# Rounded parts for the late half of u, and loads by pairs of chunks, in a decoder trunk

## The chip, the cores and the metric

The kernel runs on one core of one Trainium2 chip. The metric is the device time of one execution in microseconds (us); the time before is the median of 3 runs, 1722.25 us (1722.04 to 1727.37). The timeline and all rows come from one further execution that a hardware profiler recorded.

## What is computed

A block of a hybrid decoder for 512 tokens of width 1024: a recurrent branch (HGRN2) and a sparse-attention branch, merged by gates, then an expert layer (PEER). All values are float32. What matters here is the expert layer:

```python
def peer_ffn(x, w_q, sub_keys, u, v):          # u, v: 16384 experts x 1024
    q = (xb @ w_q).reshape(TB, H, 2, PEER_HALF)
    s = jnp.einsum('thpc,phnc->thpn', q, sub_keys)
    ...                                        # per token 8 heads x 16 experts: eidx, and softmax weights g
    ug = u[eidx]
    vg = v[eidx]
    h = jnp.einsum('tkd,td->tk', ug, xb)
    a = jax.nn.gelu(h, approximate=False) * g
    return jnp.einsum('tk,tkd->td', a, vg)
```

The result is added to the residual stream, which a last RMS norm scales.

## The kernel before, in words

The kernel is written in tile pools: each named tile has a ring of buffers, and a planner orders the instructions of each engine at build time, so an engine's order is near that of the program but not the same. On the chip every engine works through its list in order.

Up to about 460 us the kernel does the two branches and the residual. Then comes the expert layer, in two forms at once. For the first 192 tokens it **gathers**: `row` (L773) fetches, for each of the 192 slots (128 of the first block, 64 of a half block folded on 128 partitions), one row of u (`u_row`, L780: one VectorE instruction with a sum) and later one row of v (`v_row`, L792: one VectorE multiply-add into `acc`). That is 384 gathers of 512 KB, issued by GpSimd into the ring `row` of 6 buffers (L766). For the other 320 tokens (T0 on) it computes **densely** over all experts, in 128 chunks of 128 experts:

- `query` (L652) and `picks` (L689), with the first 22 chunks of u between them (from 464 to 703 us).
- The rest of the early half of u up to chunk 63 (loop at L890), with `g_group` (L860), which spreads the expert weights into a dense table `g_d` in DRAM through `stg`.
- `chunk(q)` (L987) for q = 0 to 127: loads v ahead (`v_load`), multiplies chunk q + 66 of u while there is one (`u_chunk`, L756), makes the parts of v (`v_parts`, L920), and multiplies (`v_product`, L942, and once for two chunks `v_halves`, L948). For q from 0 to 61 u and v stand together; from 62 on there is v alone, with the GELU of the early half of u read back from `h_d`.

`u_chunk` is 8 plain float32 matmuls of 320 columns; the profile has two records for each of them. `v_product` uses **rounded parts**: `hi` is v rounded to fp32r by a ScalarE copy (L925), `lo` the rest by a VectorE subtraction (L926), the same for the activations (`aH` L937, `aL` L939), and `mm3` (L74) makes three fp32r matmuls of 512 columns, L77 to L79, of them. `v_halves` is plain float32 on 64 columns of weights, 8 records for a pair of chunks.

Loads of u and wq go through the ring `u_raw` (4 buffers of 512 KB, L637), those of v through `v_raw` (8 buffers, L831), one DMA of 512 KB for each chunk, all in SyncE's queue. ScalarE's queue carries the writes and reads of `h_d`, the reads of `g_d` and small loads. The gathers are spread by `some_rows` (L803): R0, R1, R2 and R3 are the gathers for each chunk in the four stretches (2, 2, 3.2 and 0.9), with none for the last NOROW = 4 chunks of the early half; what is left is done at q = 120 (`last_rows`, L978). `issue_after` puts their instructions on VectorE behind the last `pace[0]` of the program so far.

Of the kernel before, what the change touches and what calls it, by code (L numbers as in the profile page):

```python
# [10 lines left out]
F32 = mybir.dt.float32  # L11
F32R = mybir.dt.float32r
# [6 lines left out]
OP = mybir.AluOpType  # L19
# [21 lines left out]
def trunk(ctx, tc, A, out, dbg=None):  # L41
    nc = tc.nc
    dve, act, pool, pe, sync = nc.vector, nc.scalar, nc.gpsimd, nc.tensor, nc.sync
# [70 lines left out]
    pace = [None, None]  # L114
# [11 lines left out]
    ps = psum([P, S], "hg")  # L126
# [505 lines left out]

    LEAD, UH, AHEAD = 64, [2, 2, 3, 3, 3, 3, 3, 3], 2
    UPRE = sum(UH)
    R0, R1, R2, R3, NOROW = 2, 2, 3.2, 0.9, 4
    TG, QJ, VR = 32, 4, 8
    ust = ctx.enter_context(tc.tile_pool(name="ust", reuse_waits="tile", bufs=4))  # L637

    def raw_weight(src):
        raw = ust.tile([P, 1024], F32, name="u_raw")  # L640
        sync.dma_start(raw, src)
        return raw.rearrange("p (c m) -> p c m", c=8)
# [8 lines left out]

    def query(m, w=S):  # L652

        raw = raw_weight(A["peer_wq"][m])
# [111 lines left out]
    gp = ctx.enter_context(tc.tile_pool(name="gp", reuse_waits="tile", bufs=6))  # L766
    wk = ctx.enter_context(tc.tile_pool(name="wk4", reuse_waits="tile", bufs=2))
    hh = wk.tile([P, P + HT], F32, name="hh", bufs=1)
    ah = wk.tile([P, P + HT], F32, name="ah", bufs=1)
    scr = wk.tile([P, D], F32, name="scr", bufs=1)  # L770
# [54 lines left out]
    weigh()  # L825
    rks.close()
    pps.close()


    up = ctx.enter_context(tc.tile_pool(name="up", reuse_waits="tile", bufs=2, space=PSUM))  # L830
    vt = ctx.enter_context(tc.tile_pool(name="vt", reuse_waits="tile", bufs=VR))  # L831
    with ExitStack() as st:
        gt = st.enter_context(tc.tile_pool(name="gt", reuse_waits="tile", bufs=1))
        gq = st.enter_context(tc.tile_pool(name="gq", reuse_waits="tile", bufs=2))
# [55 lines left out]
        for j in range(UPRE, LEAD):  # L890
# [13 lines left out]
    act.dma_start(gfin, bass.AP(tensor=A["norm_final"].tensor, offset=A["norm_final"].offset, ap=[[0, P], [1, D]]))  # L904
# [7 lines left out]
    raws = {}  # L912
    order = list(range(LEAD, P)) + list(range(LEAD))

    def v_load(q):
        if q < P:
            raws[q] = vt.tile([P, D], F32, name="v_raw")
            sync.dma_start(raws[q], v3[:, order[q], :])

    def v_parts(q, hgt):  # L920
        j = order[q]
        raw = raws.pop(q)
        vh = vx.tile([P, D], F32R, name="v_hi")
        vl = vx.tile([P, D], F32R, name="v_lo")
        act.copy(vh, raw)  # L925
        dve.tensor_tensor(vl, raw, vh.bitcast(F32), op=OP.subtract)  # L926
# [12 lines left out]
        pace[0] = dve.tensor_tensor(aL, gj[:, HT:], aH.bitcast(F32), op=OP.subtract)  # L939
        return gj, raw, (aH, aL), (vh, vl)  # L940
# [13 lines left out]

    def total(b, src, n):

        if n == 0:
            fin[b] = [vt.tile([P, D], F32, name="v_raw").rearrange("p (n d) -> p n d", n=2), vs.tile([P, 2], F32, name="ss")]
# [4 lines left out]
        dve.tensor_tensor(g[:, n, :], xs, gfin[:, n * 512:(n + 1) * 512], op=OP.mult)  # L963

    def finish(b):

# [10 lines left out]

    def last_rows():  # L978
        some_rows(len(rows) + len(vrows) + 1)
        for n in range(2):  # L980
            total(0, acc[0][:, n * 512:(n + 1) * 512], n)
        finish(0)

    for q in range(VR - 3):
# [28 lines left out]
    hs = vt.tile([P, D], F32, name="v_raw").rearrange("p (n d) -> p n d", n=2)  # L1013
    for n in range(2):
        act.copy(hs[:, n, :], hacc[n])
    for b in range(2):
# [100 lines left out]
```

## Time and profile before

| | before |
|---|---|
| median of the runs | 1722.25 us (1722.04 to 1727.37) |
| profiled execution: its time | 1719.29 us |
| profiled execution: span of the core | 1717.5 us |
| TensorE (PE) busy in the span | 1665.5 us, 97% |
| VectorE (DVE) busy | 1290.4 us, 75% |
| ScalarE (ACT) busy | 562.5 us, 33% |
| GpSimd (POOL) busy | 531.5 us, 31% |
| moved by DMA | 465.11 MB, mean 271 GB/s |

How to read it: the span lies within the time, with 1.8 us around it. PE is matmul, PEld the weight loads beside it. The page cuts the span into 40 slices and gives the busy share of each in tenths, PEclk the granted clock of TensorE (10 tenths is 2.4 GHz), DMA the mean share in which the 16 DMA engines had a packet. That share is counted from packet times, which overlap a little, so it can pass 1. A matmul's record is longer than its turn, since matmuls are pipelined: its pace is read from start to start.

### The profile page before, as it was taken

The numbers are of one execution on the slowest core, as the hardware profiler recorded it, in microseconds if no ns is written. First come the engines' busy times: TensorE is split into PE (matmuls) and PEld (weight loads), VectorE is DVE, ScalarE is ACT, GpSimd is POOL, SyncE is SP. The second block draws the span as 40 slices with busy tenths as digits, with TensorE's granted clock in tenths as the row PEclk, the third lists the DMA queues.
The fourth block names the chain that finished last, engine by engine and source line by source line (L and its number), as shares of the span: only waits on it lengthen the run. The fifth ranks groups of instructions, "written<-read, shape, count | busy, mean of one in ns | idle before, by whom it ended". The sixth has DMA issues, their size and how long they took to land.

```text
span 1717.5 us, 21753 instructions
## 1 busy us (share of the span) xinstructions
PE 1665.5 (97%) x7551; PEld 1181.0 (69%) x7553; DVE 1290.4 (75%) x2601; ACT 562.5 (33%) x895; POOL 531.5 (31%) x413
## 2 busy tenths in 40 slices
PE   8999999999899999899999999999999999999997
PEld 6988887778765556576776666666666666666663
DVE  4776878447369999988785787777777777888787
ACT  4422237644321111444443222222222222333333
POOL 2000000000021313255552456554454454333231
PEclk9999999999999999999999999999999999999999
DMA  6422143136665666699999999999999999999993
GB/s 231 139 74 61 62 154 105 50 108 198 200 220 201 233 212 204 216 412 417 401 393 337 346 401 381 368 347 365 362 348 365 360 346 328 361 357 341 357 351 118
DMA packets 179437, 465.11 MB, mean 271 GB/s; under 512 B 16728, under 2 KB 76504, under 8 KB 177920
## 3 DMA queue, kind: packets, MB, share of 16 engines
q1 hardware_dynamic: 52560, 200.32, 32.1%
q0 software_dynamic: 55296, 201.35, 31.2%
q10 hardware_dynamic: 71472, 62.07, 11.5%
q8 instruction: 59, 0.97, 0.2%
q14 instruction: 50, 0.41, 0.1%
HBM read 425.31 MB, written 40.39 MB: 271 GB/s over the span
## 4 chain that ended last, share of the span: by engine, by line
PE 71%; DVE 11%; DMA 9%; issue 4%; POOL 3%; ACT 1%; ACTq 0%; SPq 0%; POOLq 0%; DVEq 0%
PE ps_u L759 17%; PE acc L77 7%; PE hacc L951 7%; DMA row<-in_peer_u,eidx 7%; PE acc L78 6%; PE acc L79 6%; PE ps_mm L77 5%; PE ps_mm L79 5%; PE ps_mm L78 5%; PE ps_mm L661 2%; POOL row L776 2%; PE ps_hg L759 2%; PE ps_hg L380 2%; DVE scr L782 1%; PE ps_hg L77 1%
## 5 line engine op out<-in xcount | busy, mean ns | idle before, releaser
L759 PE MATMUL ps_u<-xfT,u_raw 128*128 128x320 f32 x1696 | 483.8, 439 | 4.3 <-ACT hg L761 4.3
L759 PEld LDWEIGHTS ps_u<-xfT,u_raw 128*128 128x128 f32 x1696 | 319.6, 192 | 150.9 <-ACT v_hi L925 20.3
L776 POOL DMA_INDIRECT row<-in_peer_u,eidx x128 | 175.7, 1372 | 319.8 <-DVE hh L782 257.9
L798 DVE SCALAR_TENSOR_TENSOR acc<-row,ah,acc 128x1024 f32<-128x1024 f32 x190 | 244.5, 1287 | 2.0
L776 POOL DMA_INDIRECT row<-in_peer_v,eidx x128 | 165.8, 1295 | 239.7 <-DVE acc L798 225.2
L77 PE MATMUL acc<-v_hi,aH 128*128 128x512 f32 x512 | 219.7, 429 | 1.2 <-ACT aH L937 1.2
L78 PE MATMUL acc<-v_lo,aH 128*128 128x512 f32 x512 | 200.7, 392 | 0.4 <-DVE v_lo L926 0.4
L79 PE MATMUL acc<-v_hi,aL 128*128 128x512 f32 x512 | 199.8, 391 | 0.0
L782 DVE CUSTOM_DVE_ANT_0 scr<-row,xf 128x1024 f32<-128x1024 f32 x128 | 156.4, 1222 | 37.2 <-DMA row<-in_peer_u,eidx 35.3
L926 DVE TENSOR_TENSOR v_lo<-v_raw,v_hi 128x1024 fp32r<-128x1024 f32 x128 | 156.0, 1220 | 36.2 <-ACT v_hi L925 35.3
L925 ACT CAST v_hi<-v_raw 128x1024 fp32r<-128x1024 f32 x128 | 134.0, 1047 | 148.8 <-PE acc L79 96.7
L761 ACT ACTIVATE hg<-ps_u 128x320 f32<-128x320 f32 x106 | 46.4, 438 | 345.0 <-PE ps_u L759 343.3
L77 PEld LDWEIGHTS acc<-v_hi,aH 128*128 128x128 f32 x512 | 96.2, 188 | 52.5 <-ACT v_hi L925 24.3
L951 PE MATMUL hacc<-v_raw,aj 128*64 128x512 f32 x512 | 126.6, 605 | 0.9 <-DVE aj L934 0.9
L109 ACT CAST w_hi<-w_raw 128x1024 fp32r<-128x1024 f32 (+3 forms) x71 | 68.3, 962 | 152.9 <-PE ps_mm L78 66.6
L71 POOL TENSOR_TENSOR rs_r<-rs_ms,half 128x1 f32<-128x1 f32 (+1 forms) x13 | 10.8, 829 | 339.7 <-DVE rs_ms L69 328.7
L78 PEld LDWEIGHTS acc<-v_lo,aH 128*128 128x128 f32 x512 | 96.4, 188 | 22.8 <-DVE v_lo L926 0.7
L661 PE MATMUL ps_mm<-xfT,u_raw 128*128 128x512 f32 (+1 forms) x288 | 111.9, 547 | 0.0
L79 PEld LDWEIGHTS acc<-v_hi,aL 128*128 128x128 f32 x512 | 96.2, 188 | 22.0 <-DVE aL L939 0.6
L776 POOL DMA_INDIRECT row<-in_peer_v,eidh x64 | 82.3, 1286 | 78.8 <-DVE acc L798 58.5
L776 POOL DMA_INDIRECT row<-in_peer_u,eidh x64 | 88.0, 1375 | 57.3 <-DVE hh L782 46.1
L77 PE MATMUL ps_mm<-xnH,w_hi 128*128 128x512 f32 (+1 forms) x248 | 100.8, 406 | 0.0
(306 smaller groups left out, 2611.3 us busy)
## 6 DMA issues: line engine op xcount, KB each, us to landing
u_raw<-in_uT SPq DMA_DIRECT2D x128, 512.0 KB
v_raw<-in_peer_v SPq DMA_DIRECT2D x128, 512.0 KB
g_d<-stg SPq DMA_DIRECT2D x10, 2048.0 KB
gj<-g_d ACTq DMA_DIRECT2D x32, 640.0 KB
w_raw<-in_wT SPq DMA_DIRECT2D x31, 512.0 KB
h_d<-hg ACTq DMA_DIRECT2D x64, 160.0 KB
hgr<-h_d ACTq DMA_DIRECT2D x64, 160.0 KB
w_raw<-in_w_out SPq DMA_DIRECT2D x16, 512.0 KB
```

The source lines that it names most:

```text
L77: pe.matmul(ps, lh, rh, start=first, stop=False, **kw)
L78: pe.matmul(ps, lh, rl, start=False, stop=False, **kw)
L79: pe.matmul(ps, ll, rh, start=False, stop=last, **kw)
L109: act.copy(hi[:, :n], raw[:, :n])
L661: pe.matmul(ps[:, ts], raw[:, c, :], xfT[:, c, ts], start=(c == 0), stop=(c == 7))
L759: pe.matmul(ps[:, :NT], raw[:, c, :], xfT[:, c, T0:], start=(c == 0), stop=(c == 7))
L776: pool.indirect_dma_start(out=g, out_offset=None, in_=A[tab], in_offset=bass.IndirectOffsetOnAxis(ap=ap, axis=0))
L782: dve.tensor_tensor_reduce(out=scr, in0=row("peer_u", half, k), in1=xfh if half else xf0, scale=1.0, scalar=0.0, op0=OP.mult, op1=OP.add, ...
L798: dve.scalar_tensor_tensor(acc[half], row("peer_v", half, k), s, acc[half], op0=OP.mult, op1=OP.add)
L925: act.copy(vh, raw)
L926: dve.tensor_tensor(vl, raw, vh.bitcast(F32), op=OP.subtract)
L951: pe.matmul(hacc[n][z * HT:(z + 1) * HT, :], gj[:, :HT], raw[:, n * 512:(n + 1) * 512], start=first, stop=last)
```

## The change

Five things change. (1) For chunks of u from 64 on, `u_chunk` makes `hi` and `lo` of the raw chunk by the new `parts` (one ScalarE copy and one VectorE subtraction of 128 x 1024, as for v) and multiplies them by `mm3` with parts of the tokens, `xfp`, which are made once behind `weigh()` (128 x 2560 on each engine): 24 fp32r matmuls of 320 columns in place of 8 plain ones. (2) u and v share one ring of parts, `w_hi` and `w_lo`, of 3 buffers each; before, `v_hi` and `v_lo` had 2 each. (3) wq, u and v are loaded by pairs of chunks, 1 MB a DMA with 8 KB on a partition, into rings of 3 pairs each; the host lays out wq and u for it. (4) The ring of gathered rows has 5 buffers in place of 6; the gathers go at R1 = 2.2, R2 = 3.0 and R3 = 1.2. (5) The last norm's gain is loaded in `last_rows` into a row buffer, in place of a tile of its own at the turn to v; `total` and `hs` use row buffers too.

```diff
-    R0, R1, R2, R3, NOROW = 2, 2, 3.2, 0.9, 4
-    TG, QJ, VR = 32, 4, 8
-    ust = ctx.enter_context(tc.tile_pool(name="ust", reuse_waits="tile", bufs=4))
+    R0, R1, R2, R3, NOROW = 2, 2.2, 3.0, 1.2, 4
+    ust = ctx.enter_context(tc.tile_pool(name="ust", reuse_waits="tile", bufs=3))
+    def raw_weight(tab, i):
+        if (tab, i // 2) not in two:
+            two[tab, i // 2] = ust.tile([P, 2, 1024], F32, name="u_raw")
+            sync.dma_start(two[tab, i // 2], A[tab][i // 2])
+        return two[tab, i // 2][:, i % 2, :]
...
     def u_chunk(j, ps):
-        raw = raw_weight(A["uT"][j])
-        for c in range(8):
-            pe.matmul(ps[:, :NT], raw[:, c, :], xfT[:, c, T0:], start=(c == 0), stop=(c == 7))
+        raw = raw_weight("uT", j)
+        if j < LEAD:
+            for c in range(8):
+                pe.matmul(ps[:, :NT], by_c(raw)[:, c, :], xfT[:, c, T0:], start=(c == 0), stop=(c == 7))
+        else:
+            hi, lo = [by_c(z) for z in parts(raw)]
+            for c in range(8):
+                mm3(ps[:, :NT], (hi[:, c, :], lo[:, c, :]), (xfp[0][:, c, :], xfp[1][:, c, :]), c == 0, c == 7)
...
-    gp = ctx.enter_context(tc.tile_pool(name="gp", reuse_waits="tile", bufs=6))
+    gp = ctx.enter_context(tc.tile_pool(name="gp", reuse_waits="tile", bufs=5))
+    def parts(raw):
+        hi = vx.tile([P, D], F32R, name="w_hi")
+        lo = vx.tile([P, D], F32R, name="w_lo")
+        act.copy(hi, raw)
+        pace[0] = dve.tensor_tensor(lo, raw, hi.bitcast(F32), op=OP.subtract)
+        return hi, lo
...
+    act.copy(xfp[0], xfT[:, :, T0:])
+    dve.tensor_tensor(xfp[1], xfT[:, :, T0:], xfp[0].bitcast(F32), op=OP.subtract)
...
-    vt = ctx.enter_context(tc.tile_pool(name="vt", reuse_waits="tile", bufs=VR))
+    vt = ctx.enter_context(tc.tile_pool(name="vt", reuse_waits="tile", bufs=3))
-    vx = ctx.enter_context(tc.tile_pool(name="vx", reuse_waits="tile", bufs=2))
+    vx = ctx.enter_context(tc.tile_pool(name="vx", reuse_waits="tile", bufs=3))
-    gfin = vs.tile([P, D], F32, name="gfin", bufs=1)
-    act.dma_start(gfin, ...)
...
     def v_load(q):
         if q < P:
-            raws[q] = vt.tile([P, D], F32, name="v_raw")
-            sync.dma_start(raws[q], v3[:, order[q], :])
+            t = v_pair()
+            sync.dma_start(t, v3[:, order[q]:order[q] + 2, :])
+            raws[q], raws[q + 1] = t[:, 0, :], t[:, 1, :]
...
     def last_rows():
         some_rows(len(rows) + len(vrows) + 1)
+        fin[0] = [gp.tile([P, D], F32, name="row")...]
+        fin["gain"] = gp.tile([P, D], F32, name="row")
+        act.dma_start(fin["gain"], ...)
...
     def chunk(q):
-        v_load(q + VR - 3)
+        if q % 2 == 0:
+            v_load(q + 4)
```

## Rows read from the trace of the kernel before

**Rows 1.** The page, parts 1 and 2: busy time and the 40 slices
```profile
PE 1665.5 (97%) x7551; PEld 1181.0 (69%) x7553; DVE 1290.4 (75%) x2601; ACT 562.5 (33%) x895; POOL 531.5 (31%) x413
DMA  6422143136665666699999999999999999999993
```

**Rows 2.** Windows: stretch, length, busy us (instructions) by engine, clock, DMA share, GB/s
```profile
740.00:800.00 60.00, 58.41 (x355) 42.84 (x354) 52.57 (x70) 26.79 (x37) 35.60 (x22) 1.00 1.03 418
...
905.00:931.00 26.00, 24.05 (x146) 18.09 (x147) 18.64 (x21) 9.84 (x13) 7.11 (x6) 0.93 0.96 370
931.00:960.00 29.00, 27.76 (x119) 19.88 (x118) 9.19 (x17) 9.95 (x15) 2.37 (x4) 1.00 0.89 283
980.00:1040.00 60.00, 60.00 (x239) 41.58 (x238) 49.06 (x80) 13.31 (x23) 35.01 (x29) 1.00 1.03 401
1000.00:1440.00 440.00, 440.00 (x1744) 299.62 (x1743) 328.08 (x396) 103.49 (x165) 232.55 (x177) 1.00 0.98 362
1460.00:1680.00 220.00, 219.64 (x927) 141.20 (x925) 180.26 (x228) 80.81 (x116) 73.97 (x56) 1.00 1.00 354
```

**Rows 3.** Timeline of PE, u and v together: start, length, engine, line, what
```profile
1300.16 1.94 PE L951 MATMUL hacc<-v_raw,aj 128*64 128x512 f32 x8
1302.03 4.57 PE L759 MATMUL ps_u<-xfT,u_raw 128*128 128x320 f32 x16
1306.20 0.63 PE L77 MATMUL acc<-v_hi,aH 128*128 128x512 f32 x1
...
1309.21 4.47 PE L759 MATMUL ps_u<-xfT,u_raw 128*128 128x320 f32 x16
...
1316.34 1.94 PE L951 MATMUL hacc<-v_raw,aj 128*64 128x512 f32 x8
```

**Rows 4.** Timeline of PE, v alone
```profile
1559.92 1.94 PE L951 MATMUL hacc<-v_raw,aj 128*64 128x512 f32 x8
...
1562.37 0.40 PE L79 MATMUL acc<-v_hi,aL 128*128 128x512 f32 x1
...
1567.17 0.39 PE L79 MATMUL acc<-v_hi,aL 128*128 128x512 f32 x1
1567.49 1.94 PE L951 MATMUL hacc<-v_raw,aj 128*64 128x512 f32 x8
```

**Rows 5.** Timeline of PE, projections: fp32r matmuls of 384 and of 290 columns
```profile
40.30 0.34 PE L78 MATMUL ps_mm<-xnL,w_hi 128*128 128x384 f32 x1
...
41.51 0.34 PE L79 MATMUL ps_mm<-xnH,w_lo 128*128 128x384 f32 x1
...
49.42 0.29 PE L77 MATMUL ps_mm<-w_hi,xnH 128*128 128x290 f32 x1
...
50.92 0.29 PE L77 MATMUL ps_hg<-w_hi,xnH 128*128 128x290 f32 x1
```

**Rows 6.** Groups of 1000 to 1440 us: busy, mean ns | idle before, releasers
```profile
L798 DVE SCALAR_TENSOR_TENSOR acc<-row,ah,acc 128x1024 f32<-128x1024 f32 x122 | 157.5, 1291 | 1.9
L926 DVE TENSOR_TENSOR v_lo<-v_raw,v_hi 128x1024 fp32r<-128x1024 f32 x55 | 67.0, 1219 | 0.0
L939 DVE TENSOR_TENSOR aL<-aj,aH 128x256 fp32r<-128x256 f32 x55 | 23.4, 425 | 25.9 <-ACT aH L937 25.0 <-issue 0.9
...
L925 ACT CAST v_hi<-v_raw 128x1024 fp32r<-128x1024 f32 x55 | 57.5, 1046 | 69.6 <-PE acc L79 68.1 <-DMA v_raw<-in_peer_v 1.4
```

**Rows 7.** Waits of 703 to 931 us: who waited for whom, total us, times, longest
```profile
DVE scr L782 <- DMA row<-in_peer_u,eidx: 25.1, 20, 4.3
```

**Rows 8.** Timeline at the turn from u to v
```profile
938.00 0.33 SPq L899 DMA_DIRECT2D g_d<-stg  x1
...
945.73 0.42 ACTq L932 DMA_DIRECT2D gj<-g_d  x1
...
953.63 1.30 DVE L934 SCALAR_TENSOR_TENSOR aj<-gj,hg 128x320 f32<-128x320 f32 x3 [1.90 <-DMA gj<-g_d]
...
954.61 0.50 PE L77 MATMUL acc<-v_hi,aH 128*128 128x512 f32 x1 [1.24 <-ACT aH L937]
```

More of the change, by code (lines that the diff above doesn't have):

```diff
@@ L634, in trunk, with by_c @@
     UPRE = sum(UH)
-    R0, R1, R2, R3, NOROW = 2, 2, 3.2, 0.9, 4
-    TG, QJ, VR = 32, 4, 8
-    ust = ctx.enter_context(tc.tile_pool(name="ust", reuse_waits="tile", bufs=4))
[L639 to L642, printed above, removed]
+    R0, R1, R2, R3, NOROW = 2, 2.2, 3.0, 1.2, 4
+    TG, QJ = 32, 4
+    ust = ctx.enter_context(tc.tile_pool(name="ust", reuse_waits="tile", bufs=3))
+    two = {}
+    def raw_weight(tab, i):
[3 more added lines that the diff above has]
+        return two[tab, i // 2][:, i % 2, :]
+    def by_c(w):
+        return w.rearrange("p (c m) -> p c m", c=8)
     rks = ExitStack()
@@ L652, in query @@
     def query(m, w=S):
-        raw = raw_weight(A["peer_wq"][m])
+        raw = by_c(raw_weight("peer_wq", m))
         kT = rk.tile([P, P], F32, name="kT", bufs=3)
@@ L764, in u_chunk @@
         return hgt
-    gp = ctx.enter_context(tc.tile_pool(name="gp", reuse_waits="tile", bufs=6))
+    gp = ctx.enter_context(tc.tile_pool(name="gp", reuse_waits="tile", bufs=5))
     wk = ctx.enter_context(tc.tile_pool(name="wk4", reuse_waits="tile", bufs=2))
+    xfp = []
+    def parts(raw):
[4 more added lines that the diff above has]
+        return hi, lo
     hh = wk.tile([P, P + HT], F32, name="hh", bufs=1)
@@ L827, in trunk @@
     pps.close()
+    xhl = ctx.enter_context(tc.tile_pool(name="xhl", reuse_waits="tile", side="right", bufs=1))
+    xfp = [xhl.tile([P, 8, NT], F32R, name="xf" + k) for k in "HL"]
+    act.copy(xfp[0], xfT[:, :, T0:])
+    dve.tensor_tensor(xfp[1], xfT[:, :, T0:], xfp[0].bitcast(F32), op=OP.subtract)
     up = ctx.enter_context(tc.tile_pool(name="up", reuse_waits="tile", bufs=2, space=PSUM))
-    vt = ctx.enter_context(tc.tile_pool(name="vt", reuse_waits="tile", bufs=VR))
+    vt = ctx.enter_context(tc.tile_pool(name="vt", reuse_waits="tile", bufs=3))
     with ExitStack() as st:
@@ L900, in trunk @@
             some_rows(R1 if j < LEAD - NOROW else 0)
-    vx = ctx.enter_context(tc.tile_pool(name="vx", reuse_waits="tile", bufs=2))
+    vx = ctx.enter_context(tc.tile_pool(name="vx", reuse_waits="tile", bufs=3))
     vs = ctx.enter_context(tc.tile_pool(name="vs", reuse_waits="tile", bufs=2))
-    gfin = vs.tile([P, D], F32, name="gfin", bufs=1)
-    act.dma_start(gfin, bass.AP(tensor=A["norm_final"].tensor, offset=A["norm_final"].offset, ap=[[0, P], [1, D]]))
     vp = ctx.enter_context(tc.tile_pool(name="vp", reuse_waits="tile", bufs=1, space=PSUM))
@@ L913, in trunk, with v_pair @@
     order = list(range(LEAD, P)) + list(range(LEAD))
+    def v_pair():
+        return vt.tile([P, 2, D], F32, name="v_raw")
     def v_load(q):
         if q < P:
-            raws[q] = vt.tile([P, D], F32, name="v_raw")
-            sync.dma_start(raws[q], v3[:, order[q], :])
+            t = v_pair()
+            sync.dma_start(t, v3[:, order[q]:order[q] + 2, :])
+            raws[q], raws[q + 1] = t[:, 0, :], t[:, 1, :]
     def v_parts(q, hgt):
@@ L922, in v_parts @@
         raw = raws.pop(q)
[L923 to L926, printed above, removed]
+        vh, vl = parts(raw)
         if hgt is None:
@@ L955, in total @@
     def total(b, src, n):
-        if n == 0:
-            fin[b] = [vt.tile([P, D], F32, name="v_raw").rearrange("p (n d) -> p n d", n=2), vs.tile([P, 2], F32, name="ss")]
+        if b not in fin:
+            fin[b] = [gp.tile([P, D], F32, name="row").rearrange("p (n d) -> p n d", n=2), vs.tile([P, 2], F32, name="ss")]
         g, ss = fin[b]
@@ L962, in total @@
         act.activation(scr[:, n * 512:(n + 1) * 512], xs, AF.Square, accum_out=ss[:, n:n + 1])
-        dve.tensor_tensor(g[:, n, :], xs, gfin[:, n * 512:(n + 1) * 512], op=OP.mult)
+        dve.tensor_tensor(g[:, n, :], xs, fin["gain"][:, n * 512:(n + 1) * 512], op=OP.mult)
     def finish(b):
@@ L979, in last_rows @@
         some_rows(len(rows) + len(vrows) + 1)
+        fin[0] = [gp.tile([P, D], F32, name="row").rearrange("p (n d) -> p n d", n=2), vs.tile([P, 2], F32, name="ss")]
+        fin["gain"] = gp.tile([P, D], F32, name="row")
+        act.dma_start(fin["gain"], bass.AP(tensor=A["norm_final"].tensor, offset=A["norm_final"].offset, ap=[[0, P], [1, D]]))
         for n in range(2):
@@ L982, in last_rows @@
         finish(0)
-    for q in range(VR - 3):
+    for q in (0, 2):
         v_load(q)
     def chunk(q):
-        v_load(q + VR - 3)
+        if q % 2 == 0:
+            v_load(q + 4)
         if LEAD + AHEAD + q < P:
@@ L1012, in trunk @@
     v_halves(lasts, False, True)
-    hs = vt.tile([P, D], F32, name="v_raw").rearrange("p (n d) -> p n d", n=2)
+    hs = gp.tile([P, D], F32, name="row").rearrange("p (n d) -> p n d", n=2)
     for n in range(2):
@@ L1077, in layouts @@
         "peer_u": c(i["peer_u"][0]),
-        "uT": c(i["peer_u"][0].reshape(P, P, 8, P).transpose(1, 3, 2, 0).reshape(P, P, 1024)),
+        "uT": c(i["peer_u"][0].reshape(P, 64, 2, 8, P).transpose(1, 4, 2, 3, 0).reshape(64, P, 2, 1024)),
         "peer_v": c(i["peer_v"][0]),
         "keysT": c(i["peer_keys"][0].transpose(3, 1, 0, 2).reshape(P, 16, P)),
-        "peer_wq": np.stack([kc(i["peer_wq"][0][:, m * P:(m + 1) * P]) for m in range(16)]),
+        "peer_wq": np.stack([np.stack([kc(i["peer_wq"][0][:, m * P:(m + 1) * P]) for m in (k, k + 1)], axis=1)
+                             for k in range(0, 16, 2)]),
         "w_up": np.stack([np.concatenate([kc(i[n][0][:, m * P:(m + 1) * P]) for n in ("w_up_a", "w_up_b")], axis=1)
```

## The prediction, made before any run of the change

> **What bounds the kernel now.** I read the page first, then the windows of each stretch, then the timeline of one steady pair of chunks, and last the waits. The page says that PE is busy 97% of the span, but also that the DMA engines are full from slice 18 on [rows 1]. The windows keep both: with u and v together (1000 to 1440 us) PE is busy 440 of 440 us, DMA has a share of 0.98 at 362 GB/s and DVE is busy 328.08 us; with v alone (1460 to 1680 us) PE has 219.64 of 220 us and DMA 1.00 at 354 GB/s [rows 2]. The timeline decides which of the two bounds. From one `v_halves` to the next are 16.18 us with u and v, and 7.57 us with v alone [rows 3, 4]; between them PE's instructions stand back to back. So PE is the bound and DMA keeps up, without much to spare. Only before the turn does DVE stand still for a gathered row, 25.1 us in 20 waits [rows 7], at 418 GB/s and a share of 1.03 [rows 2].
>
> **Part 1, the late u in fp32r parts.** A pair of chunks costs 16.18 us with its two chunks of u and 7.57 us without, so one plain chunk of u costs (16.18 - 7.57) / 2 = 4.30 us [rows 3, 4]. The new one has 24 fp32r matmuls of 320 columns, of which the trace has none. The bounds are the steps at 290 columns, (50.92 - 49.42) / 11 = 0.136 us, and at 384, (41.51 - 40.30) / 7 = 0.173 us [rows 5]; between them by columns, 320 take 0.148 us. That is 24 x 0.148 = 3.55 us, with 3.27 and 4.15 us as ends. A chunk saves 0.75 us, and a pair of chunks falls to 16.18 - 1.50 = 14.68 us if PE stays the bound. The step at 512 columns is (1567.17 - 1562.37) / 21 = 0.229 us [rows 4]. The Trainium skill, in "TensorE: Matmul & The Clock Gate", section "Back-to-back issue gap", gives columns / 2.4 + 2.5 ns, which is 216 ns at 512 columns and so shorter than the row; by it, as an estimate, the new chunk would take 3.26 us and save 1.04 us. The rows decide.
>
> From q = 0 to 61 there are 31 pairs, 64 chunks of u in all. The first four chunks bring nothing: the last part of `g_d` is issued at 938.00 us, its read at 945.73, it lands at 953.6, and the first v product starts at 954.61 [rows 8]. What PE saves before that it waits. So 30 pairs x 1.50 us = 45 us are what PE alone would give.
>
> DVE gets one subtraction more for each chunk. Now it is busy 328.08 / 440 x 16.18 = 12.06 us a pair [rows 2]. Two subtractions of 1.22 us come to it, and 0.4 gathered rows of 1.29 us go (R2 from 3.2 to 3.0) [rows 6]: 12.06 + 2.44 - 0.52 = 13.98 us, 95% of 14.68. It also waits for ACT's `aH` ahead of `aL`, 25.0 us in 440, which is 0.92 us a pair [rows 6]; its wait for the GELU is for PE and goes away when PE is ahead. With that wait DVE needs 14.90 us, a little over PE. I take 14.90 us: DVE becomes the bound by a hair. The ends are 14.68 us (the wait is filled with other work) and 15.6 us (below). Gain: (16.18 - 14.90) x 30 = 38 us.
>
> ACT gets a copy of 1.05 us for each chunk [rows 6]; it is busy 103.49 of 440 us [rows 2], so this is hidden, at about 40%. The parts of the tokens are 2.5 times as wide as a part of v, so 2.6 us on ACT and 3.1 us on DVE, once, at the start of the G stretch, where DVE is nearly full: I count 1 us, with 0 and 3 as ends.
>
> **Part 2, one ring of three.** The copy for the next u now waits until PE has done with the v product two parts before. Behind that copy on ACT stand the next GELU and `aH`; who waits is DVE's subtraction, the gathered rows queued behind it, and then PE. The cover is one u and one v product, 3.55 + 12 x 0.229 = 6.3 us, against 1.05 + 1.22 us for the two steps and up to three rows of 1.29 us queued ahead of the subtraction, 6.1 us together [rows 4, 6]. It fits, just. I count 0; if a fourth row stands in between, some 1.1 us go per chunk, which is the second rival.
>
> **Part 3, pairs of loads.** The same bytes go in half the DMAs. SyncE now waits for two chunks to be free, with 6 chunks of u and 6 of v held in place of 4 and 8; in the late half the raw chunk of u is free after DVE and not after PE. No row shows what a 1 MB load costs beside gathers; the ends are a wait that PE feels and somewhat better packets. No load of v is late by more than 1.4 us in all in the stretch [rows 6], so I take 0.
>
> **Part 4, the gathers.** What R2 gives back the others take. R1 adds 0.2 for each of 38 chunks, 7.6 rows of 0.524 MB or 4.0 MB, in a stretch already at 418 GB/s [rows 2]: 9.5 us if all of it shows, 0 if the room behind it (370 and 283 GB/s up to 960 us [rows 2]) takes it. The rows stand in DVE's order ahead of the work PE waits for, and there is one buffer fewer, so I count 5 us. At R3 = 1.2, some 64 rows are left (384 - 44 - 83.6 - 192), spread over 53 chunks or 27 pairs. A pair moves 7.57 us x 354 GB/s = 2.68 MB now and 0.6 x 0.524 = 0.31 MB more then; to stay at 7.57 us DMA must move 396 GB/s. The ends are today's 354 GB/s (8.46 us a pair, 24 us in all) and 401 GB/s, which the stretch from 980 to 1040 us reached with a share of 1.03 [rows 2] (0). This stretch has more small transfers than that one, but the rate seen there is above the need: I take a third, 8 us.
>
> **Part 5, the gain's load** leaves the turn, where it went between two steps of the chain through `g_d`, and goes to q = 120, where DVE may wait for 512 KB with three pairs of v behind it. Up to 1.4 us gained and 3 us lost (about 1.3 us of transfer at 400 GB/s [rows 2], and its latency): 0.
>
> **Sum**, on the profiled execution: 1719.29 - 38 + 5 + 8 + 1 = 1695 us. The median of the runs is 3 us above that execution, so 1698 us.
>
> **Rivals.** *PE alone decides (0.17).* DVE's wait is filled, the extra gathers find room: 45 us less and 2 us of costs, 1722 - 43 = 1679 us. For it: the steady 16.18 us under a DMA share of 0.98. Against it: DVE at 95%, more than in any window of rows 2.
>
> *DMA is the ceiling (0.15), the one that ends slower.* If the rates of today are all there is, PE's room can't be used: a pair with u moves 16.18 x 362 = 5.86 MB, less 0.21 MB for 0.4 rows, 5.65 MB at 362 GB/s, 15.6 us, a gain of only 17 us; v alone loses 24 us and the G stretch 9.5 us. That is 16 us slower, 1738 us. It decides as long as the rates can rise by less than about 2%; at 2.4% gain and loss balance. For it: shares of 0.98 to 1.03 everywhere. Against it: a pair of 14.68 us needs 385 GB/s, and 401 and 418 GB/s were moved [rows 2]. The Trainium skill, in "DMA: Bandwidth & Descriptors", section "Specifications", sets a limit of about 358 GB/s of HBM for a core, which speaks against this change; by it a pair with u would take 15.8 us. The 401 GB/s of a stretch that mostly reads do not agree with it.
>
> *The chain of the parts (0.14).* DVE's in-order list and the ring of three cost about 1.1 us a chunk: the pair stays near 16 us, nothing is gained there but some 7 us, and the 14 us of parts 1 and 4 remain: about 1722 + 7 = 1729 us at its worst and 1712 us where half of the chunks pay; I set it at 1720 us.
>
> *The change doesn't do what it says (0.04)*: the planner orders u late, or the first parts wait for memory that `stg` still holds at the turn: PE stands still for up to 8 us more there, 1706 us.
>
> **How the numbers follow.** The forecast has 0.50, at 1698 us, its own range 1686 to 1712 us (a pair from 14.7 to 15.2 us, parts 4 from 5 to 20 us). A measurement of this kernel tells a difference of about 0.3%, 5 us. Faster by more than that (under 1717 us): the forecast, PE alone, 0.04 for the turn and a quarter of the chain, 0.74 in all. Within 0.3%: half of the chain and a third of the ceiling, 0.12. Slower: the rest, 0.14. The range from 1676 to 1728 us leaves out most of the ceiling's 0.15 and a little of PE alone.
>
> **What would show it.** Right: fp32r steps of about 0.148 us at 320 columns, a steady pair of 14.7 to 15.2 us up to q = 61 with DVE over 90%, and 385 GB/s or more there; with v alone a pair of 7.6 to 8.2 us while gathers last. Wrong: a pair above 15.5 us, with DVE waiting for rows (the ceiling) or PE waiting for `lo` while DVE has idle time (the chain); or the G stretch longer than 10 us more.

## The result, and the profile after

The changed kernel takes 1741.52 us (median of 20 runs, 1726.55 to 1750.88) against 1727.41 us before (20 runs beside it): a ratio of 1.0085, 95% interval 1.0064 to 1.0106. It is slower by 0.85%, where 1698 us and faster was forecast, and the time lies outside the range of 1686 to 1712 us. The forecast stood on a median of 1722.25 us for before, so as a ratio it said 0.986. The profiled execution took 1740.18 us.

The page of after, parts 1 and 2 (busy time, and the 40 slices), which answer to [rows 1]:

```profile
PE 1639.5 (94%) x8063; PEld 1223.8 (70%) x8065; DVE 1355.7 (78%) x2666; ACT 618.7 (36%) x960; POOL 564.8 (32%) x413
PEclk9899999999999999999898999999999999899999
DMA  7321243135554656699998899999999999899993
```

PE is busy 26 us less than before and the span is 21 us longer: PE's own work shrank as meant, and its idle time grew by 47 us, from 52.0 to 98.9 us. To find where, I cut both traces at the same instructions: the weight load of the first matmul with wq, the first one-hot step of `g_group`, the last matmul into `ps_g`, the first v product, the last GELU of u, the last `v_halves`. The table holds the lengths in us, worked out from those instructions' starts; G is the stretch in which the table `g_d` is made.

| stretch | before | after | difference |
|---|---|---|---|
| up to the first matmul with wq | 457.7 | 464.4 | +6.7 |
| projections and picks, first 22 chunks of u | 255.0 | 260.3 | +5.3 |
| G: table `g_d`, rest of the early u | 223.2 | 252.6 | +29.4 |
| turn | 18.7 | 18.4 | -0.3 |
| u and v together | 488.5 | 456.0 | -32.5 |
| v alone | 254.6 | 267.5 | +12.9 |
| tail | 19.8 | 19.3 | -0.5 |

The first row is hardly the change: rates_alone (below), which leaves that work as it was, stands at 462.4 us there, and all 13 other traces of this case lie between 461.9 and 466.5 us. The profiled execution of before was an early one. So 32.5 us were won where the forecast put its gain, and 47.6 us were lost in the three other stretches where rows are gathered.

**The gain.** PE's timeline of after, between 1200 and 1351 us (start, length, engine, line, what); it answers to [rows 3]:

```profile
1209.50 0.31 PE L78 MATMUL ps_u<-xfL,w_hi 128*128 128x320 f32 x1
...
1211.26 0.31 PE L78 MATMUL ps_u<-xfL,w_hi 128*128 128x320 f32 x1
...
1291.69 1.94 PE L975 MATMUL hacc<-v_raw,aj 128*64 128x512 f32 x8
...
1306.28 1.94 PE L975 MATMUL hacc<-v_raw,aj 128*64 128x512 f32 x8
...
1320.87 1.94 PE L975 MATMUL hacc<-v_raw,aj 128*64 128x512 f32 x8
```

Between the first two rows lie 12 steps: 1.76 / 12 = 0.147 us for 320 columns. A pair of chunks takes 14.59 us (16.18 before [rows 3]) over most of the stretch. The groups of 1000 to 1440 us (busy, mean ns | idle before, what ended it), which answer to [rows 6], show the subtractions of u and v with no idle time before them, and DVE waiting for rows:

```profile
L818 DVE SCALAR_TENSOR_TENSOR acc<-row,ah,acc 128x1024 f32<-128x1024 f32 x112 | 143.6, 1282 | 15.0 <-DMA row<-in_peer_v,eidh 8.1 <-DMA row<-in_peer_v,eidx 5.1
...
L785 DVE TENSOR_TENSOR w_lo<-v_raw,w_hi 128x1024 fp32r<-128x1024 f32 x59 | 71.9, 1219 | 0.0
L785 DVE TENSOR_TENSOR w_lo<-u_raw,w_hi 128x1024 fp32r<-128x1024 f32 x59 | 71.9, 1218 | 0.0
```

**The loss in G.** Windows of G (stretch, length, busy us and instructions of PE, PEld, DVE, ACT, POOL, granted clock, DMA share, GB/s), first before, then after:

```profile
703.00:931.00 228.00, 217.28 (x1279) 159.38 (x1278) 187.10 (x250) 96.03 (x130) 119.29 (x77) 0.99 0.98 380
```

```profile
720.00:980.00 260.00, 224.77 (x1282) 163.14 (x1280) 191.88 (x251) 100.69 (x132) 133.50 (x84) 0.93 0.93 348
```

The work is the same, 1279 and 1282 matmul records. It took 32 us longer: PE's idle time went from 10.7 to 35.2 us, and its busy time grew by 7.5 us, since the mean granted clock fell from 0.99 to 0.93. The DMA engines were less full than before: a share of 0.93 at 348 GB/s, where it was 0.98 at 380. The waits of after in that window name the chain (who waited for whom, us in all, times, longest); the first answers to [rows 7]:

```profile
DVE scr L802 <- DMA row<-in_peer_u,eidx: 46.9, 21, 5.1
...
PE ps_g L905 <- DVE ow L897: 32.3, 9, 8.2
```

Before, PE waited less for `ow`, a factor of the table's matmuls:

```profile
PE ps_g L881 <- DVE ow L873: 10.3, 4, 3.6
```

One piece of DVE's timeline in after, and the PE row that waits for it, show how the one becomes the other (in brackets: idle time before, and what ended it):

```profile
852.18 1.22 DVE L802 CUSTOM_DVE_ANT_0 scr<-row,xf 128x1024 f32<-128x1024 f32 x1 [2.19 <-DMA row<-in_peer_u,eidx]
...
856.82 1.23 DVE L802 CUSTOM_DVE_ANT_0 scr<-row,xf 128x1024 f32<-128x1024 f32 x1 [3.41 <-DMA row<-in_peer_u,eidx]
...
866.89 1.23 DVE L897 TENSOR_TENSOR ow<-oz,wp 128x2048 f16<-128x2048 f16 x1
```

```profile
868.17 1.89 PE L905 MATMUL ps_g<-ow,oz 128*128 128x128 f16 x16 [8.18 <-DVE ow L897]
```

The gathered rows stand in DVE's list ahead of `ow`. A row that lands late holds `ow`, and PE stands idle 8.18 us. Beside such gaps the granted clock falls to its lower level, 1.2 GHz, for a while: from 943 to 950 us, where a wait of PE of 7.57 us ends, it is 0.50, and the window from 931 to 960 us has a mean of 0.82 (all of G before: 0.99). Windows of after, in the columns above:

```profile
931.00:960.00 29.00, 21.43 (x109) 15.52 (x108) 19.94 (x28) 8.56 (x11) 15.99 (x11) 0.82 0.93 349
1000.00:1440.00 440.00, 433.64 (x2355) 351.78 (x2354) 397.99 (x485) 162.00 (x238) 253.79 (x180) 1.00 0.98 372
1480.00:1680.00 200.00, 193.65 (x796) 122.91 (x797) 170.05 (x213) 68.92 (x100) 86.02 (x60) 0.98 1.00 364
```

**The loss in v alone.** Over the whole stretch (1451.60 to 1719.10 us in after, 1443.10 to 1697.70 before) PE is idle for 14.1 us, before for 1.3, which is nearly all of the 12.9 us. The last row above has a share of 1.00 at 364 GB/s, and PE idle for 6.35 us. There DVE waits for the read of the GELU, `hgr`, which travels among the rows. The wait from 1480 to 1680 us, first before, then in after, and one place of it in the timelines of DVE and PE; the two `hacc` rows, 18.56 us apart, answer to [rows 4], where they stand 7.57 us apart:

```profile
DVE aj L934 <- DMA hgr<-h_d: 9.9, 7, 2.7
```

```profile
DVE aj L958 <- DMA hgr<-h_d: 23.0, 8, 7.3
```

```profile
1481.78 0.49 DVE L958 SCALAR_TENSOR_TENSOR aj<-gj,hgr 128x320 f32<-128x320 f32 x1 [7.25 <-DMA hgr<-h_d]
```

```profile
1469.80 1.94 PE L975 MATMUL hacc<-v_raw,aj 128*64 128x512 f32 x8
1482.76 0.79 PE L77 MATMUL acc<-w_hi,aH 128*128 128x512 f32 x1 [8.04 <-ACT aH L961]
1488.36 1.94 PE L975 MATMUL hacc<-v_raw,aj 128*64 128x512 f32 x8
```

Five things were changed at once, so the trace says where, not yet which of them.

### The profile page after: what moved, and what is told of

Same layout as the page of the kernel before. It is cut to its first block, busy times and chain, and to the rows that moved or that the text cites. A ratio compares the mean times of both kernels' runs of the same rounds, so it can differ in the third digit from the quotient of the medians.

```text
span 1738.4 us, 22617 instructions
## 1 busy us (share of the span) xinstructions
PE 1639.5 (94%) x8063; PEld 1223.8 (70%) x8065; DVE 1355.7 (78%) x2666; ACT 618.7 (36%) x960; POOL 564.8 (32%) x413
## 3 DMA queue, kind: packets, MB, share of 16 engines
q1 hardware_dynamic: 32976, 200.31, 30.5%
q10 hardware_dynamic: 71472, 62.07, 11.4%
q8 instruction: 63, 1.03, 0.2%
## 4 chain that ended last, share of the span: by engine, by line
PE 30%; DMA 28%; issue 19%; DVE 14%; POOL 7%; ACT 1%; ACTq 0%; POOLq 0%; SPq 0%; DVEq 0%
DMA row<-in_peer_u,eidx 9%; POOL row L796 6%; DMA hgr<-h_d 6%; PE ps_mm L77 5%; PE ps_mm L79 5%; DMA row<-in_peer_u,eidh 5%; PE ps_mm L78 5%; DMA row<-in_peer_v,eidh 4%; DMA row<-in_peer_v,eidx 3%; DVE acc L818 3%; DVE w_lo L785 2%; PE ps_u L766 2%; DVE scr L802 2%; PE ps_hg L380 2%; PE ps_hg L77 1%
## 5 line engine op out<-in xcount | busy, mean ns | idle before, releaser
L77 PE MATMUL acc<-w_hi,aH 128*128 128x512 f32 x512 | 206.4, 403 | 9.8 <-ACT aH L961 9.8
L78 PE MATMUL acc<-w_lo,aH 128*128 128x512 f32 x512 | 204.1, 399 | 8.1 <-DVE w_lo L785 7.7
L766 PE MATMUL ps_u<-xfT,u_raw 128*128 128x320 f32 x672 | 199.8, 452 | 6.8 <-ACT hg L772 6.8
L79 PE MATMUL acc<-w_hi,aL 128*128 128x512 f32 x512 | 202.5, 396 | 2.5 <-DVE aL L963 2.4
L766 PEld LDWEIGHTS ps_u<-xfT,u_raw 128*128 128x128 f32 x672 | 130.3, 199 | 57.6 <-ACT hg L772 7.3
L785 DVE TENSOR_TENSOR w_lo<-v_raw,w_hi 128x1024 fp32r<-128x1024 f32 x128 | 156.0, 1220 | 13.7 <-ACT w_hi L784 13.6
L77 PE MATMUL ps_u<-xfH,w_hi 128*128 128x320 f32 x512 | 162.8, 318 | 2.8 <-ACT w_hi L784 2.7
L784 ACT CAST w_hi<-v_raw 128x1024 fp32r<-128x1024 f32 x128 | 133.8, 1049 | 81.6 <-DMA v_raw<-in_peer_v 26.6
L79 PE MATMUL ps_u<-xfH,w_lo 128*128 128x320 f32 x512 | 159.2, 311 | 1.4 <-DVE w_lo L785 1.4
L78 PE MATMUL ps_u<-xfL,w_hi 128*128 128x320 f32 x512 | 159.3, 311 | 0.0
## 6 DMA issues: line engine op xcount, KB each, us to landing
g_d<-stg SPq DMA_DIRECT2D x10, 2048.0 KB, 12.9
gj<-g_d ACTq DMA_DIRECT2D x32, 640.0 KB, 12.9
```

Source lines behind the costliest of these rows:

```text
L77: pe.matmul(ps, lh, rh, start=first, stop=False, **kw)
L78: pe.matmul(ps, lh, rl, start=False, stop=False, **kw)
L79: pe.matmul(ps, ll, rh, start=False, stop=last, **kw)
L766: pe.matmul(ps[:, :NT], by_c(raw)[:, c, :], xfT[:, c, T0:], start=(c == 0), stop=(c == 7))
L784: act.copy(hi, raw)
L785: pace[0] = dve.tensor_tensor(lo, raw, hi.bitcast(F32), op=OP.subtract)
```

## The experiments

Theory A, the forecast's: the parts bring some 38 us and the other edits cost little each; then one of them must be far dearer than its term. Rival B: DMA has no more to give (the forecast's slower rival), so PE's saving can't be used. Rival C: the loads by pairs delay the gathers. Rival D: the fifth row buffer in place of the sixth delays them. Each experiment has runs of the kernel before beside it, and its ratio is to those. Stretches are cut as in the table.

### Parts of the change alone, on the kernel before

**pair_alone**, wq, u and v by pairs:

```diff
-    ust = ctx.enter_context(tc.tile_pool(name="ust", reuse_waits="tile", bufs=4))
+    ust = ctx.enter_context(tc.tile_pool(name="ust", reuse_waits="tile", bufs=3))
...
+            two[tab, i // 2] = ust.tile([P, 2, 1024], F32, name="u_raw")
+            sync.dma_start(two[tab, i // 2], A[tab][i // 2])
...
-    vt = ctx.enter_context(tc.tile_pool(name="vt", reuse_waits="tile", bufs=VR))
+    vt = ctx.enter_context(tc.tile_pool(name="vt", reuse_waits="tile", bufs=3))
...
+            sync.dma_start(t, v3[:, order[q]:order[q] + 2, :])
```

> The kernel before with one part of the change alone: wq, u and v loaded by pairs of chunks (1 MB a load, rings of 3 pairs); the last sums use row buffers. Rates, six row buffers and plain float32 u as before. The stretch in which the table is made (from the first one-hot instruction of VectorE to the last table matmul; 223 us before, 253 us after) tells the theories apart. Loads theory (1 MB loads crowd out the gathers, VectorE stands in its list for a late row): the stretch takes 240 to 255 us and the whole 1735 to 1750 us. Rates theory and buffers theory: 221 to 227 us there, the whole within 5 us of the kernel before.

Measured: 1727.39 us, ratio 1.0000 (0.9979 to 1.0021). G takes 222.0 us, v alone 254.8 us, as before. By themselves the pairs cost nothing that these runs could tell: rival C falls in its simple form.

**rates_alone**, the gathers' rates:

```diff
-    R0, R1, R2, R3, NOROW = 2, 2, 3.2, 0.9, 4
+    R0, R1, R2, R3, NOROW = 2, 2.2, 3.0, 1.2, 4
```

> The kernel before with the rates of the gathers of the kernel after alone (R1 2.2, R2 3.0, R3 1.2). Rates theory (7.6 more gathers than the DMA engines can bring in the table stretch): the stretch takes 235 to 255 us instead of 223, and the stretch with v alone gets 5 to 13 us longer, the whole 1735 to 1755 us. Loads theory and buffers theory: the table stretch stays under 230 us, the whole within 8 us of the kernel before.

Measured: 1744.43 us, ratio 1.0091 (1.0054 to 1.0127). G is 12.5 us longer (235.7), v alone 10 us (264.5); u and v together stay at 488.5. In v alone the share is 1.00 at 358 GB/s (1480 to 1640 us), and from 1480 to 1680 us `aj` waits 24.6 us for `hgr`, the same wait as in after:

```profile
1480.00:1640.00 160.00, 150.81 (x615) 97.02 (x615) 130.67 (x162) 53.53 (x77) 65.76 (x47) 0.97 1.00 358
```

**row5_alone**, one row buffer fewer:

```diff
-    gp = ctx.enter_context(tc.tile_pool(name="gp", reuse_waits="tile", bufs=6))
+    gp = ctx.enter_context(tc.tile_pool(name="gp", reuse_waits="tile", bufs=5))
```

> The kernel before with five buffers for gathered rows instead of six, nothing else. Buffers theory (five rows in flight bring fewer rows in the time, since each takes about 15 us to land in the table stretch): the table stretch takes 235 to 255 us instead of 223, the whole 1733 to 1755 us. The other two theories: under 228 us, the whole within 5 us of the kernel before.

Measured: 1740.79 us, ratio 1.0075 (1.0050 to 1.0101), so 14 us for one buffer of 512 KB. It costs in every stretch with gathers but the one of u and v: 3.6 us in projections and picks, 5.7 us in G, 4.2 us in v alone. The whole came as the theory had it, but spread: G stays below the 235 us that it expected. The records of VectorE and TensorE stand in the same order as in the kernel before, all 2601 and 7551 of them, so this is waiting and no other plan. In G the time from the issue of a gather to its use is 11.4 us (median), with six buffers 13.5 us: with five, GpSimd can run that much less ahead. A gather lands there after 10.6 us (median, 720 to 980 us), not after the 15 us that was expected.

**pair_row5**, the edits of pair_alone and row5_alone together:

```diff
-    gp = ctx.enter_context(tc.tile_pool(name="gp", reuse_waits="tile", bufs=6))
+    gp = ctx.enter_context(tc.tile_pool(name="gp", reuse_waits="tile", bufs=5))
...
+            sync.dma_start(two[tab, i // 2], A[tab][i // 2])
...
+            sync.dma_start(t, v3[:, order[q]:order[q] + 2, :])
```

> The kernel before with loads by pairs and five row buffers together, plain float32 u and the rates of before. Alone the pairs cost 1 us and the fifth buffer 14 us. If the two only add: 1738 to 1744 us, table stretch 228 to 232 us. If a 1 MB load matters just because fewer gathers stand beside it: 1750 us or more, table stretch 236 us or more.

Measured: 1749.02 us, ratio 1.0120 (1.0083 to 1.0158). That is between the two times expected. The two are 23 us together, 14 and 0 alone. So the pairs cost some 8 us beside five buffers, though the intervals of this ratio and of row5_alone's overlap; projections and picks take 263.6 us (row5_alone: 258.5), G 234.1 (228.9).

### Parts of the change undone, from after

**after_single**, loads of one chunk in rings of the same bytes (6 buffers of 512 KB each):

```diff
-            two[tab, i // 2] = ust.tile([P, 2, 1024], F32, name="u_raw")
-            sync.dma_start(two[tab, i // 2], A[tab][i // 2])
+        raw = ust.tile([P, 1024], F32, name="u_raw")
+        sync.dma_start(raw, A[tab][i // 2][:, i % 2, :])
...
-            t = v_pair()
-            sync.dma_start(t, v3[:, order[q]:order[q] + 2, :])
+            raws[q] = vt.tile([P, D], F32, name="v_raw")
+            sync.dma_start(raws[q], v3[:, order[q], :])
```

> The kernel after with the loads of wq, u and v one chunk at a time again (512 KB each, rings of 6 chunks, the same memory). Loads theory: the table stretch falls from 253 to 223 to 232 us while the stretch with u and v keeps its 456 us, so the whole is 1705 to 1720 us. Rates theory and buffers theory: the table stretch stays at 245 us or more, the whole at 1732 us or more.

Measured: 1725.09 us, ratio 0.9985 (0.9969 to 1.0000). That lies between the two branches of what was expected, in G too. In after the pairs cost 16 us by the medians. The two profiled executions lie 9 us apart, nearly all of it in G (252.6 and 243.9 us); where the rest goes, one trace of each can't tell.

**after_R**, the rates of before in after (pairs and five buffers stay):

```diff
-    R0, R1, R2, R3, NOROW = 2, 2.2, 3.0, 1.2, 4
+    R0, R1, R2, R3, NOROW = 2, 2, 3.2, 0.9, 4
```

> The kernel after with the rates of the kernel before (R1 2, R2 3.2, R3 0.9); five row buffers and loads by pairs stay. If what the runs so far show adds up (rates alone cost 12 us in the table stretch and 10 us with v alone), the table stretch falls from 253 to 238 to 243 us and the stretch with v alone from 267 to 256 to 260 us, the whole to 1715 to 1725 us. If the loss in the table stretch needs only one of its causes to be there, the stretch stays at 248 us or more. VectorE limits the stretch with u and v (my sum before: 14.9 us a pair at R2 = 3.0, 0.26 us more at 3.2): then that stretch grows from 456 to 464 us or more; TensorE limits it: 454 to 458 us.

Measured: 1741.98 us, ratio 1.0079 (1.0051 to 1.0107): no gain at all. G falls to 238.4 us as it should, but u and v together take 471.0 us in place of 456.0. With R2 back at 3.2 the 14 us that left G reappear there. What was expected would read this as VectorE's limit at R2 = 3.2; but with the same rate and single loads the stretch takes 468.2 us with five row buffers, 451.0 with six and 445.9 with seven (parts_row5, parts_alone and parts_row7, below), so the rate alone is no limit. Where rows are short of buffers, moving them moves the loss.

**single_row6**, after_single with six row buffers, four chunks of u (wq too) and six of v:

```diff
-    ust = ctx.enter_context(tc.tile_pool(name="ust", reuse_waits="tile", bufs=6))
+    ust = ctx.enter_context(tc.tile_pool(name="ust", reuse_waits="tile", bufs=4))
...
-    gp = ctx.enter_context(tc.tile_pool(name="gp", reuse_waits="tile", bufs=5))
+    gp = ctx.enter_context(tc.tile_pool(name="gp", reuse_waits="tile", bufs=6))
```

> The kernel after with single loads, a ring of 4 chunks of u and 6 of v, and six row buffers; the rates of the kernel after stay. Buffers theory: against single loads with five row buffers (table stretch 244 us, v alone 269 us) the table stretch falls to 236 to 240 us and v alone to 262 to 266 us, the whole to 1710 to 1718 us. Rates theory alone: no change, 1722 to 1728 us.

Measured: 1702.59 us, ratio 0.9860 (0.9823 to 0.9897), better than expected: the sixth buffer gives back 22.5 us against after_single, though that one held two chunks more of u. Most of it comes in u and v together (455.5 to 445.4 us) and in G (243.9 to 233.8 us).

### The parts alone, and the row buffers beside them

**parts_alone**, the parts of u and the ring of three, single loads (u 4, v 6), six row buffers, the rates of before (the gain's load and the last tiles as in after):

```diff
+            hi, lo = [by_c(z) for z in parts(raw)]
+                mm3(ps[:, :NT], (hi[:, c, :], lo[:, c, :]), (xfp[0][:, c, :], xfp[1][:, c, :]), c == 0, c == 7)
```

> The rounded parts of u and the shared ring of three parts alone: single loads (4 chunks of u, 6 of v in the ring), six row buffers, the rates of the kernel before. If gathers (rates and buffers) are all that ate the gain: table stretch 223 to 228 us, u and v 454 to 460 us, v alone 254 to 258 us, the whole 1692 to 1702 us, faster than the kernel before by 25 to 34 us. If the parts themselves cost something in the table stretch (their 3 us on VectorE, the shared memory) or if VectorE limits u and v at R2 = 3.2: 1706 us or more.

Measured: 1695.12 us, ratio 0.9834 (0.9809 to 0.9859), 30.5 us less than before, as expected; u and v together take 451.0 us. Part 1 of the forecast is real.

**parts_row5** and **parts_row7**, the same kernel with five and with seven row buffers (the line of five is shown):

```diff
-    gp = ctx.enter_context(tc.tile_pool(name="gp", reuse_waits="tile", bufs=6))
+    gp = ctx.enter_context(tc.tile_pool(name="gp", reuse_waits="tile", bufs=5))
```

> The parts alone (single loads, rates of the kernel before; 1695 us with six row buffers) with five row buffers. Buffers theory: the loss is that of the buffer in the kernel before, 14 us, or more, since the parts leave VectorE less idle time to make up for a late row: 1708 to 1720 us, the table stretch 232 to 240 us, u and v 455 to 465 us. If the sixth buffer only matters beside the rates of the kernel after: under 1700 us.

> The parts alone with seven row buffers (a ring of 4 chunks of u, 6 of v, single loads, rates of the kernel before). Buffers theory, if the table stretch still stands for rows with six: table stretch 220 to 224 us instead of 226, v alone 255 to 258 us instead of 260, the whole 1685 to 1692 us. If six are enough: 1693 to 1697 us.

Measured: 1722.45 us (0.9961, 0.9935 to 0.9988) and 1681.66 us (0.9739, 0.9712 to 0.9767). Both lie beyond what the buffers theory expected, on its side. One knob, 5, 6 and 7 buffers, gives 1722, 1695 and 1682 us. VectorE's records (2666) stand in the same order with five as with six, and so do TensorE's from the first matmul with wq on (5689). With seven both orders are those of six up to 1654 us of parts_alone; they differ in the last 40 us, around the last rows. The windows from 1000 to 1400 us, first with five, then with seven:

```profile
1000.00:1400.00 400.00, 384.80 (x2077) 311.00 (x2076) 362.65 (x446) 145.16 (x213) 238.89 (x168) 0.99 1.01 379
```

```profile
1000.00:1400.00 400.00, 399.96 (x2196) 327.87 (x2195) 379.00 (x452) 153.46 (x221) 253.06 (x177) 1.00 1.03 398
```

With five buffers the waits of that window have 24.8 us of DVE for rows, and PE waits behind:

```profile
PE acc L78 <- DVE w_lo L784: 14.9, 8, 3.8
...
DVE scr L801 <- DMA row<-in_peer_u,eidh: 11.1, 10, 2.9
...
DVE acc L817 <- DMA row<-in_peer_v,eidh: 7.3, 9, 1.5
DVE acc L817 <- DMA row<-in_peer_v,eidx: 6.4, 7, 1.6
```

With seven the same three row waits are 7.6 us:

```profile
DVE scr L801 <- DMA row<-in_peer_u,eidh: 2.9, 4, 1.6
DVE acc L817 <- DMA row<-in_peer_v,eidh: 2.5, 2, 1.4
DVE acc L817 <- DMA row<-in_peer_v,eidx: 2.2, 3, 1.1
```

PE waits for nothing there: it is busy 399.96 of 400 us, while DVE is busy 95%. This decides rival B for this stretch, too: DMA moved 398 GB/s for 400 us, where the rival allowed 362. parts_row7 is the fastest version here, ahead of both kernels.

### The pairs beside six row buffers

**parts_upair**, parts_alone with u and wq by pairs (3 of 1 MB), which leaves room for five single chunks of v:

```diff
-        raw = ust.tile([P, 1024], F32, name="u_raw")
-        sync.dma_start(raw, A[tab][i // 2][:, i % 2, :])
+            two[tab, i // 2] = ust.tile([P, 2, 1024], F32, name="u_raw")
+            sync.dma_start(two[tab, i // 2], A[tab][i // 2])
...
-    vt = ctx.enter_context(tc.tile_pool(name="vt", reuse_waits="tile", bufs=6))
+    vt = ctx.enter_context(tc.tile_pool(name="vt", reuse_waits="tile", bufs=5))
```

> The parts alone with six row buffers and the rates of the kernel before, and wq and u loaded by pairs (a ring of 3 pairs; v singly, a ring of 5). In the kernel before, loads by pairs cost nothing with six row buffers. If that holds here too: table stretch 224 to 229 us, the whole 1692 to 1700 us. If loads of 1 MB delay the gathers whatever the buffers: table stretch 232 us or more, the whole 1703 us or more.

Measured: 1705.31 us, ratio 0.9867 (0.9832 to 0.9901), between what was expected. G is 226.6 us, as in parts_alone (226.3), so the pairs of u don't hurt it; but v alone takes 270.1 us against 259.8. There ACT's `w_hi` waits for v (51.7 us, 31 times), where v has one buffer fewer:

```profile
ACT w_hi L784 <- DMA v_raw<-in_peer_v: 51.7, 31, 7.1
```

That wait alone doesn't tell much: from 1480 to 1700 us it is 29.9 us (13 times, longest 3.3) in parts_alone. Whether the pairs or the smaller ring of v did that, this kernel alone can't tell.

**parts_vpair**, parts_alone with v by pairs in 3 buffers of 1 MB, the same bytes:

```diff
-            raws[q] = vt.tile([P, D], F32, name="v_raw")
-            sync.dma_start(raws[q], v3[:, order[q], :])
+            t = v_pair()
+            sync.dma_start(t, v3[:, order[q]:order[q] + 2, :])
```

> parts_alone (single loads, 6 row buffers, rates of before: 1695.1 us) with one thing changed: v is loaded by pairs of chunks into 3 buffers of 1 MB, the same bytes held as its 6 of 512 KB. Six row buffers stay. Theory (the pairs cost something only where the gathered rows are short of buffers): 1692 to 1700 us, v alone 257 to 263 us. Rival (pairs of v cost of themselves once u stands in parts, as the 10 us more of v alone in parts_upair could be read): 1703 us or more, v alone 265 us or more; then the 10 us there were not its ring of five single chunks alone.

Measured: 1692.58 us, ratio 0.9812 (0.9777 to 0.9847); v alone 259.6 us. The pairs of v cost nothing where there are six row buffers, although `w_hi` waits 46.7 us for v there (19 times, longest 4.8). The 10 us in parts_upair then point to its ring of five chunks of v, since no chunk of u is loaded in that stretch; a kernel with that ring alone was not run, so this is argued.

### The sum of the pieces

Built up one step at a time, each median against the one above it (single_row6 and after_single also differ by two chunks more of u held):

| version | us | step |
|---|---|---|
| before, beside parts_alone | 1725.6 | |
| parts_alone: parts, ring of three | 1695.1 | -30.5 |
| single_row6: and the new rates | 1702.6 | +7.5 |
| after_single: and five row buffers | 1725.1 | +22.5 |
| after: and loads by pairs | 1741.5 | +16.4 |

The steps hold in this order alone: on the kernel before, the new rates cost 16 to 18 us (rates_alone), the fifth buffer 14 and the pairs 0.

## Why the prediction was wrong

**The step that failed** is the price of the gathers and of what stands beside them. Part 4 counted 13 us for rates and row buffer, 5 in G and 8 in v alone; in the order of the table above they cost 30.0 us. Part 3 counted 0 for the pairs; they cost 16.4 us beside five row buffers. Part 1 brought 30.5 us where 37 were counted. The prediction's own sign of being wrong came with it: "the G stretch longer than 10 us more" is 29.4 us.

**Part 1 was right.** The forecast interpolated 0.148 us for a step of 320 columns; it is 0.147 us. "A pair of chunks falls to ... 14.68 us if PE stays the bound": 14.59 us. The forecast then took 14.90 us, because DVE's work and its wait for `aH` came to that. That sum did not bind: with seven buffers, and R2 at 3.2, DVE is busy 379.00 of 400 us and PE is never late. The gain of 38 us was 32.5 us in after and 37.5 us in parts_alone (488.5 to 451.0). The one subtraction and copy more for each chunk are hidden, and the ring of three cost nothing in that window: with seven buffers PE has no wait for `w_lo` there.

**Part 4 failed, in its row buffer.** The forecast wrote: "The rows stand in DVE's order ahead of the work PE waits for, and there is one buffer fewer, so I count 5 us", for rates and buffer together, and in G alone. The mechanism is the one that then ruled; the size is wrong. The buffer alone costs 14 us on the kernel before (row5_alone), 27 us beside the parts (parts_row5) and 22.5 us beside the parts with the new rates. Three things were missed. The bytes that R1 adds, from which I took 9.5 us, don't bound the cost: what a late row costs is PE's idle time behind `ow`, and the lower clock after it. It acts in every stretch with gathers, the projections too, for which the sum had no term. And [rows 7] showed DVE waiting 25.1 us for rows with six buffers, which I read as a matter of rates. Beside the parts six were already too few, since a seventh brought 13 us; the kernel before was not run with seven.

**R1 and R3.** R1 cost 12.5 us in G alone, above the upper end of 9.5 us. For R3 I asked for a rate between 354 and 401 GB/s and took two thirds of the way up, 8 us; v alone stayed at 358 (rates_alone, 160 us) to 364 GB/s (after, 200 us), at a share of 1.00, and lost 10 to 13 us, so this term was only a little small. The bound was right, the reading of the 401 GB/s too hopeful: that was a stretch of 60 us, and the best 60 us that were found in v alone moved 389 GB/s (after_single, 1485 to 1545 us).

**Part 3, the pairs, was right alone and wrong in company.** 0 was counted; pair_alone gives 0.8 us with an interval across zero, parts_vpair shows no loss either. Beside five row buffers they cost 8 us (pair_row5) and 16 us in after. What passes between a load of 1 MB and the gathers there is not shown by any run, and the cause stays open. It is no later landing of the typical row: from 720 to 980 us the median gather of u lands after 11.0 us in after and 10.8 us in after_single, while DVE waits 46.9 and 38.9 us for rows. That no cost appears beside six buffers is shown for the pairs on the kernel before and for those of v beside the parts. I read it as one shortage counted twice, but that is argued.

**The rivals.** *DMA is the ceiling* said 1738 us, close to the time measured, but for another reason, so that is luck: it left u and v together a gain of 17 us, and there 32.5 us were gained and 398 GB/s moved in parts_row7; in G the share fell to 0.93. Its reason comes nearest to holding in v alone, and there it had 24 us where 12.9 were lost. The Trainium skill, in "HBM Reference", section "Specifications (TRN2)", says that a core streaming alone measures about 425 GB/s, well above its share of 358; the 398 GB/s here agree with that, and the limit that the prediction quoted was the wrong one of the two for a kernel on one core. *The chain of parts* does appear in parts_row5 (PE waits 14.9 us for `w_lo`), but it is fed by late rows and is gone with seven buffers. *PE alone decides* did not come for this change. parts_row7 comes near its time, 1681.66 us where that rival said 1679, but as another kernel: single loads, the rates of before and seven row buffers.

**Part 5** stays at nothing: the turn takes 18.4 us against 18.7, the tail 19.3 against 19.8.

So the gain was in place, and was given back by the 5.3, 29.4 and 12.9 us more in the stretches around it.

## What to carry to other kernels

When a change pays for buffers with the buffers of another ring, price that ring by its waits: a DVE that already waits 25 us for gathered rows has none to give, and in an in-order list each late row stands ahead of somebody else's work. Ask of a lost buffer in how many stretches the ring is in use, not only in the one that looks full. An edit that costs nothing alone can cost beside another (14 and 0 us became 23; in after the pairs cost 16), so a sum of terms needs its worst pair beside it.

## What was not expected of the hardware

One buffer of 512 KB in a ring of gathers moved the whole kernel by 27 us (five to six) and by 13 us (six to seven), while the DMA engines had a share of 1.01 with five and 1.03 with seven from 1000 to 1400 us. Loads of 1 MB with 8 KB on a partition in place of 512 KB with 4 KB brought the kernel before nothing: the ratio is 1.0000 (pair_alone). The Trainium skill, in "DMA: Bandwidth & Descriptors", section "Measured (HBM→SBUF, 128 partitions, SWDGE, issued from GpSimd)", advises batches of 1 MiB and more; no run here shows a gain by it where many DMAs are under way at once.
